# Row groups of 1, 3, 4 and 8 row tiles in place of 4, 6 and 6 in the first projection of a hybrid decoder block

## The chip, the cores and the metric

The kernel runs on one core of a Trainium2 chip. The time is device microseconds of one execution, from launch to the last write; the profile's span runs from the first to the last instruction of one execution that the hardware profiler recorded. Engines: PE (matrix multiplication; PEld are its weight loads), DVE (vector), ACT (scalar), POOL (GpSimd), SP (issues most of the DMA transfers). Each engine runs its own instructions in order and waits on semaphores for the others.

## The reference

One decoder block on x (256 x 2048, float32), with a conditioning vector c. What matters here is its start:

```python
c_act = jax.nn.silu(c)
mod = c_act @ w_ada + b_ada                      # 2048 -> 6 * 2048
sh1, sc1, g1, sh2, sc2, g2 = jnp.split(mod, 6)
h = rms_norm(x, norm_mix_g) * (1.0 + sc1) + sh1
proj = h @ w_in                                  # 2048 -> 8192
u, q, k, v, ga, gb = jnp.split(proj, [1024, 2048, 3072, 4096, 6144])
```

Behind it come an S5 state-space branch on u, attention on q, k and v, a merge gated by sigmoid(ga) and sigmoid(gb), a projection w_out, a second modulated norm, and an MLP of 2048 x 8192 with squared ReLU; at the end a last norm. Everything is float32; the output is 256 x 2048.

## The kernel before

Matrix products keep float32 accuracy by splitting: a weight tile (128 rows of the matrix by 1024 columns, 512 KB) is loaded into `wraw`, ACT casts it to `whi` (L161) and DVE subtracts to get the rest, `wlo` (L163). The activations are split in the same way (`ah`, `al`; the trace calls both `ah`). Three matmuls then make one product: high by high (L208, L261), high by the activations' low (L209, L263), low by high (L210, L265). `wraw` has 7 buffers, `whi` and `wlo` have 4 each, so a cast of weight tile n waits for PE to be done with tile n - 4. `stream` (L167) gives out the split tiles of a unit one after the other.

The rows of w_in are cut into 16 row tiles of 128, which stand for 128 channels of h each. A row tile of h (`make_h1`, L495: `htmp` on ACT, then a split into `ah`) can only be made when its 128 columns of sc1 and sh1 are known: sums over c_act times w_ada. For row tiles 0 to 3 these sums are matmuls (`ada_first`, L272: four loads of 512 KB, tiles named `adap` and `adac` in the trace, a column of `A` and one of `B`). For row tiles 4 to 15 they are wide sums on DVE (`ada_wide`, L351, recorded at L367; tile `ahm`, 128 x 2048, two loads each), four for a pair of row tiles. There are 24 of them. The buffers go round: from the thirteenth on, the load of a wide sum may start when the sum two before it has ended (the table `free`).

So that PE needn't wait for all of h, the first stage is cut into units: a unit is one block of 1024 output columns (0: q, 1: k, 2: v, 3: u, 4: the first half of ga) over the row tiles of one or two groups, accumulated in four PSUM banks. `GR` gives the sizes of the groups. A unit over a later group starts from what the earlier one left: its four banks are emptied by copies (L1066) and the next unit of that block is seeded by four copies back into PSUM (`seeded`, L192). Five banks go round between the units. `gemm_t` (units 0, 1, 3) and `gemm_n` (2, 4) run the matmuls; a row tile of a unit is called a tile here, and the stage has 80 of them, 0 to 79. At the end of each tile, `step` (L138) runs the side work that stands in lanes: "second" (row tiles 1 to 3), "ada" (wide sums), "xr" (scaling x), "ssm" (tables of the state-space branch on DVE, ACT and PE). `want` (L1110) runs out of turn what is needed for the next row tile.

With (4, 6, 6) the units are q, k, v, u over row tiles 0 to 3, ga over 0 to 9, u, v, k over 4 to 9, q over 4 to 15, and ga, u, k, v over 10 to 15. In the first unit each of the row tiles 1 to 3 is made between two tiles of q (`follow`, L1022), and eight matmuls that nobody reads (`idle`, L126, tile `unread`) run while its input is made.

The program is written once and ordered by a list scheduler with priorities (`high_priority`) and extra order edges (`after`); so the order on each engine is that of the built program, shown below.

Of the kernel before, what the change touches and what calls it, by code (L numbers as in the profile page):

```python
# [41 lines left out]
OF1 = 3000  # L42
# [13 lines left out]
RS3 = .7  # L56
GR = (4, 6, 6)
RAT = 1.5
# [19 lines left out]
class Kern:  # L78
    def __init__(self, ctx, tc, a, out):
# [14 lines left out]
        self.done = []  # L94
        self.want = lambda kt: None

    def hot(self):
# [69 lines left out]
    def stream(self, src, kts, c0, homes=()):  # L167
        homes = list(homes)
        for kt in kts:
# [17 lines left out]
            self.step()  # L187

    def seeded(self, banks, seed):
        for o, d in zip(banks, seed or ()):  # L190
            with self.tc.high_priority(offset=OFF):
                self.nc.scalar.copy(*d(o))  # L192
        return bool(seed)

    def gemm_t(self, src, kts, c0, xh, xl, koff=0, mid={}, homes=(), seed=None):
        nc = self.nc
        banks = self.four("pt")
        full = self.seeded(banks, seed)
        n = len(kts)
        for i, (kt, hi, lo) in enumerate(self.stream(src, kts, c0, homes)):  # L200
            kx = kt - koff
# [38 lines left out]
    def gemm_n(self, src, kts, c0, xh, xl, koff=0, tail=1, mid={}, homes=(), seed=None):  # L240
# [4 lines left out]
        held, prev = [], None  # L245
        for i, unit in enumerate(self.stream(src, kts, c0, homes)):
            u = (i,) + unit
# [689 lines left out]
    def body(self):  # L937
# [52 lines left out]
        def modn(kt, home=None, gates=(None, None)):  # L990
            return (self.ada_first(1, kt, fin_scale(1, A1, lambda: self.gmix, kt, 1), home and home[0:2], gates[0]),
                    self.ada_first(0, kt, fin_shift(0, B1, kt, 1), home and home[2:4], gates[1]))

        def totals(parts):
            for units, fold, last in parts:
                for ld, tot in units:
                    tot()
            for units, fold, last in parts:
                fold(parts[1][2]())
# [20 lines left out]
        homes = {1: regs[0:4], 2: regs[4:8], 3: [h[:, i, :] for h in h4 for i in range(2)]}  # L1020

        def follow(kt):  # L1022
            def f():
                with self.tc.high_priority(offset=OF1):
                    parts = modn(kt, homes[kt], (self.mid, self.mm))
                    for units, fold, last in parts:
                        for ld, tot in units:
                            ld()
                    self.scale1(kt, n=1)
                    totals(parts)  # L1030
                    self.idle(8)
                    self.make_h1(kt, A1, B1, 1)
                    self.gates = [(None, self.acopy)] + ([(None, self.done[-1][1])] * 3 if kt == 3 else [])
            return f
        self.early = False
        self.qk = self.slot("S1", [P, 2, 8, S], name="qk")
# [52 lines left out]

        def qkvu(which, g0, g1):  # L1090
            kts = range(groups[g0][0], sum(groups[g1]))
            c0 = (1024, 2048, 3072, 0, 4096)[which]
            f = self.gemm_n if which in (2, 4) else self.gemm_t
            evac(which, f(win, kts, c0, self.ah, self.al, seed=seeds(which) if g0 else None), g0)

# [33 lines left out]
        self.drain = drain  # L1129
        self.lane("second", [follow(kt) for kt in (1, 2, 3)], 1.0)  # L1130
        self.lane("xr", [nop] * 3 + [lambda k0=k0: self.scale1(k0, self.done[-1][0]) for k0 in range(4, KT, 2)], .5)
        jobs = self.ringed(units, free)
        self.lane("ada", [nop] * 3 + jobs[0:1] + [nop] * 2 + jobs[1:] + late, R1)
        self.lane("ssm", [nop] * SL + self.ssm_builds(), 1.0)
        for u in ((0, 0, 0), (1, 0, 0), (2, 0, 0), (3, 0, 0), (4, 0, 1), (3, 1, 1), (2, 1, 1), (1, 1, 1), (0, 1, 2),
                  (4, 2, 2), (3, 2, 2)):
            qkvu(*u)
            if u == (4, 0, 1):
                self.lanes["ssm"][1] = SR1
# [4 lines left out]
        self.bias_load()  # L1144
        qkvu(1, 2, 2)
        qkvu(2, 2, 2)
        ga = self.ga
# [390 lines left out]
```

## Time and profile before

| | us |
|---|---|
| median of 3 runs (lowest, highest) | 1383.23 (1383.08, 1383.5) |
| the profiled execution | 1383.14 |
| its span | 1381.3 |
| PE, DVE, ACT busy | 1352.4, 1043.7, 741.1 |
| end of q's unit (tile 55 of the 80) | 202.9 |
| mean granted clock of PE | 0.996 |

A row of the order of time gives the start and the length in us, the engine, the line, the operation with output and inputs, the shapes, the count and, in brackets, how long the engine sat idle before it and what ended that. A row of a stretch gives the bounds, the length, each engine's busy time with its count of instructions, the granted clock of PE (1.00 is full), the share of the DMA engines and GB/s. A row of the waits gives who waited for whom: the total, the number and the longest in us.

### The profile page before, as it was taken

To read this page: it belongs to the slowest core of one execution; us is meant where nothing else is said; L and a number is where in the kernel's file an instruction comes from. 1 tells how busy PE (TensorE), PEld (TensorE's weight loads), DVE (VectorE), ACT (ScalarE), POOL (GpSimd) and SP (SyncE) were. 2 spreads that over 40 slices of the span, in tenths; PEclk is the share of its full clock that TensorE was granted. 3 is DMA by queue.
4 is the path that set the end of the run, shared out by engine and by line. 5 is a ranking of instruction groups with operands and counts; after the bars stand their busy time and mean duration, and the time that the engine had idled before them with its cause. 6 is when DMAs were issued, how large, how long until landed. Compare 5 with 4: busy or idle time off the path is not lost.

```text
span 1381.3 us, 21633 instructions
## 1 busy us (share of the span) xinstructions
PE 1352.4 (98%) x8338; PEld 1173.9 (85%) x8338; DVE 1043.7 (76%) x1449; ACT 741.1 (54%) x1020; POOL 42.6 (3%) x96
## 2 busy tenths in 40 slices
PE   6999999999999999999999999999999999999997
PEld 5888899988888887888999888888888888888885
DVE  6699987687898898988886976777666555555676
ACT  4466658656557643446565655444453554634543
POOL 1000000500003000000000000000000000000000
PEclk9999999999999999999999999999999999999999
DMA  9999965898447889898697878788878656566561
GB/s 371 387 400 371 354 206 176 263 333 280 164 160 235 298 294 341 294 391 290 212 361 242 284 248 251 244 251 286 246 240 242 200 189 197 188 190 195 179 202 64
DMA packets 112423, 356.43 MB, mean 258 GB/s; under 512 B 12240, under 2 KB 12272, under 8 KB 111904
## 3 DMA queue, kind: packets, MB, share of 16 engines
q1 hardware_dynamic: 109280, 348.96, 74.5%
q0 software_dynamic: 2896, 5.83, 1.4%
q8 instruction: 65, 1.06, 0.3%
q10 hardware_dynamic: 144, 0.26, 0.1%
q14 instruction: 38, 0.31, 0.1%
HBM read 350.79 MB, written 2.51 MB: 256 GB/s over the span
## 4 chain that ended last, share of the span: by engine, by line
PE 59%; DVE 3%; DMA 1%; ACT 1%; issue 1%; DVEq 0%; ACTq 0%
PE pd L226 13%; PE pn L261 11%; PE pn L263 11%; PE pn L265 11%; PE pd L230 7%; PE pt L208 2%; PE pt L210 2%; PE pt L209 2%; DVE wraw L325 1%; DMA wraw<-in_w_proj_ssm_dram 1%; DVE wlo L163 1%; DMA wraw<-in_w_out_dram 0%; DMA wraw<-in_w_ff_dram 0%; ACT whi L161 0%; PE trm L1232 0%
## 5 line engine op out<-in xcount | busy, mean ns | idle before, releaser
L161 ACT CAST whi<-wraw 128x1024 fp32r<-128x1024 f32 x448 | 467.6, 1051 | 516.7 <-PE pn L263 228.4
L163 DVE TENSOR_TENSOR wlo<-wraw,whi 128x1024 fp32r<-128x1024 f32 x448 | 545.2, 1223 | 253.4 <-ACT whi L161 248.5
L226 PE MATMUL pd<-h2h,whi 128*128 128x512 f32 x800 | 208.9, 393 | 0.0
L261 PE MATMUL pn<-whi,ff 128*128 128x512 f32 x496 | 193.0, 389 | 0.0
L263 PE MATMUL pn<-whi,ff 128*128 128x512 f32 x496 | 193.0, 389 | 0.0
L265 PE MATMUL pn<-wlo,ff 128*128 128x512 f32 x496 | 191.6, 389 | 0.0
L226 PEld LDWEIGHTS pd<-h2h,whi 128*128 128x128 f32 x800 | 140.5, 189 | 21.7
L325 DVE SCALAR_TENSOR_TENSOR wraw<-wraw,cb 128x1024 f32<-128x1024 f32 x128 | 156.2, 1221 | 0.0
L261 PE MATMUL pn<-whi,ah 128*128 128x512 f32 x320 | 126.3, 397 | 2.3 <-ACT ah L161 1.6
L230 PEld LDWEIGHTS pd<-h2h,wlo 128*128 128x128 f32 x800 | 116.1, 190 | 12.5
L263 PE MATMUL pn<-whi,ah 128*128 128x512 f32 x320 | 125.2, 391 | 0.0
L230 PE MATMUL pd<-h2h,wlo 128*128 128x256 f32 x800 | 119.3, 281 | 0.0
L265 PE MATMUL pn<-wlo,ah 128*128 128x512 f32 x320 | 115.1, 393 | 0.0
L208 PE MATMUL pt<-ah,whi 128*128 128x256 f32 x384 | 106.3, 287 | 6.4 <-ACT ah L161 4.7
L265 PEld LDWEIGHTS pn<-wlo,ff 128*128 128x128 f32 x496 | 93.1, 188 | 19.4
L261 PEld LDWEIGHTS pn<-whi,ff 128*128 128x128 f32 x496 | 93.1, 188 | 19.2
L263 PEld LDWEIGHTS pn<-whi,ff 128*128 128x128 f32 x496 | 93.1, 188 | 19.0
L209 PE MATMUL pt<-ah,whi 128*128 128x256 f32 x384 | 108.3, 287 | 0.0
L210 PE MATMUL pt<-ah,wlo 128*128 128x256 f32 x384 | 103.4, 285 | 0.0
L208 PEld LDWEIGHTS pt<-ah,whi 128*128 128x128 f32 x384 | 73.2, 194 | 7.6 <-ACT ah L161 5.4
L209 PEld LDWEIGHTS pt<-ah,whi 128*128 128x128 f32 x384 | 74.2, 193 | 1.3 <-issue 0.8
L261 PEld LDWEIGHTS pn<-whi,ah 128*128 128x128 f32 x320 | 60.0, 188 | 15.0 <-ACT ah L161 1.8
(378 smaller groups left out, 2016.8 us busy)
## 6 DMA issues: line engine op xcount, KB each, us to landing
wraw<-in_w_ff_dram SPq DMA_DIRECT2D x256, 512.0 KB, 4.8
wraw<-in_w_in_dram SPq DMA_DIRECT2D x128, 512.0 KB, 6.3
wraw<-in_wat_dram SPq DMA_DIRECT2D x128, 512.0 KB, 5.6
ahm<-in_wat_dram SPq DMA_DIRECT2D x48, 512.0 KB, 7.2
wraw<-in_w_out_dram SPq DMA_DIRECT2D x32, 512.0 KB, 6.4
wraw<-in_w_proj_attn_dram SPq DMA_DIRECT2D x16, 512.0 KB, 6.2
wraw<-in_w_proj_ssm_dram SPq DMA_DIRECT2D x16, 512.0 KB, 6.0
ahm<-in_wan_dram SPq DMA_DIRECT2D x8, 512.0 KB, 11.6
```

The source lines that it names most:

```text
L161: h = self.nc.scalar.copy(hi, src)
L163: s = self.nc.vector.tensor_sub(lo, src, hi.bitcast(F32))
L208: nc.tensor.matmul(o, hi[:, c], xh[:, kx, :], start=st, stop=False, skip_group_check=True)
L209: nc.tensor.matmul(o, hi[:, c], xl[:, kx, :], start=False, stop=False, skip_group_check=True)
L210: self.mm = nc.tensor.matmul(o, lo[:, c], xh[:, kx, :], start=False, stop=sp, skip_group_check=True)
L226: nc.tensor.matmul(banks[blk], hi[:, cut(blk, k)], x2[:, ks[k], :, :], start=i + k == 0, stop=False, skip_group_check=True)
L230: self.mm = nc.tensor.matmul(banks[blk][:, S:2 * S], lo[:, cut(blk, k)], x2[:, ks[k], 0, :], start=False, stop=last and k == 1, skip_group ...
L261: nc.tensor.matmul(o, xh[:, kx, tk], hi[:, c], start=q == 0 and not full, stop=False, skip_group_check=full)
L263: nc.tensor.matmul(o, xl[:, kx, tk], hi[:, c], start=False, stop=False, skip_group_check=full)
L265: self.mm = last = nc.tensor.matmul(o, xh[:, kx, tk], lo[:, c], start=False, stop=q == n - 1, skip_group_check=full)
L325: v.scalar_tensor_tensor(w, w, 1.0, self.cb[:, (i % 2) * 1024:(i % 2 + 1) * 1024], op0=OP.mult, op1=OP.mult, accum_out=pc[:, i:i + 1])
```

## The change

The groups are now 1, 3, 4 and 8 row tiles. Five units begin on the first row tile: q, k, v, u over row tile 0 alone (tiles 0 to 3) and ga over row tiles 0 to 3 (tiles 4 to 7). Then u, v, k over row tiles 1 to 3 (8 to 16), q over 1 to 7 (17 to 23), k, v, u over 4 to 7 (24 to 35), ga over 4 to 15 (36 to 47), and q, u, k, v over 8 to 15 (48 to 79). There are 17 units in place of 13, and twelve of them are seeded in place of nine. The making of row tiles 1 to 3 is spread: `follow` sums, `finish` folds and makes the row tile a tile later; the unread matmuls are gone. And `prime` takes the next unit's first weight tile (load and split) ahead of the copies that empty the banks of the unit before.

```diff
-GR = (4, 6, 6)
+GR = (1, 3, 4, 8)
+    def prime(self, *args):
+        gen = self.stream(*args)
+        self.primed = (next(gen), gen)
+
+    def flow(self, *args):
+        if self.primed:
+            first, gen = self.primed
+            self.primed = None
+            yield first
+        else:
+            gen = self.stream(*args)
+        yield from gen
 ...
-        for i, (kt, hi, lo) in enumerate(self.stream(src, kts, c0, homes)):
+        for i, (kt, hi, lo) in enumerate(self.flow(src, kts, c0, homes)):
 ...
+        sums = {}
+
         def follow(kt):
             def f():
                 with self.tc.high_priority(offset=OF1):
-                    parts = modn(kt, homes[kt], (self.mid, self.mm))
-                    for units, fold, last in parts:
-                        for ld, tot in units:
-                            ld()
+                    sums[kt] = modn(kt, homes[kt], (self.mid if kt < 3 else self.mm, self.mm))
+                    for i in range(2):
+                        for units, fold, last in sums[kt]:
+                            for job in units:
+                                job[i]()
+            return f
+
+        def finish(kt):
+            def f():
+                with self.tc.high_priority(offset=OF1):
+                    for units, fold, last in sums[kt]:
+                        fold(self.mm)
                     self.scale1(kt, n=1)
-                    totals(parts)
-                    self.idle(8)
                     self.make_h1(kt, A1, B1, 1)
-                    self.gates = [(None, self.acopy)] + ([(None, self.done[-1][1])] * 3 if kt == 3 else [])
             return f
 ...
+        def qkvu(u, after=None):
+            which, g0, g1 = u
             f = self.gemm_n if which in (2, 4) else self.gemm_t
-            evac(which, f(win, kts, c0, self.ah, self.al, seed=seeds(which) if g0 else None), g0)
+            banks = f(*place(*u), self.ah, self.al, seed=seeds(which) if g0 else None)
+            if after:
+                self.prime(*place(*after))
+            evac(which, banks, g0)
 ...
-        self.lane("second", [follow(kt) for kt in (1, 2, 3)], 1.0)
+        self.lane("second", [follow(1), both(finish(1), follow(2)), finish(2), nop, follow(3), finish(3)], 1.0)
 ...
-        for u in ((0, 0, 0), (1, 0, 0), (2, 0, 0), (3, 0, 0), (4, 0, 1), (3, 1, 1), (2, 1, 1), (1, 1, 1), (0, 1, 2),
-                  (4, 2, 2), (3, 2, 2)):
-            qkvu(*u)
-            if u == (4, 0, 1):
+        order = [(0, 0, 0), (1, 0, 0), (2, 0, 0), (3, 0, 0), (4, 0, 1), (3, 1, 1), (2, 1, 1), (1, 1, 1), (0, 1, 2),
+                 (1, 2, 2), (2, 2, 2), (3, 2, 2), (4, 2, 3), (0, 3, 3), (3, 3, 3)]
+        for u, after in zip(order, order[1:] + [None]):
+            qkvu(u, after)
+            if u == (0, 1, 2):
                 self.lanes["ssm"][1] = SR1
 ...
-        qkvu(1, 2, 2)
-        qkvu(2, 2, 2)
+        qkvu((1, 3, 3), (2, 3, 3))
+        qkvu((2, 3, 3))
```

The order on the engines, at three places. A row has the line, the operation, output and inputs, and the shape; x2 stands for two in a row. Line numbers of the changed kernel are 14 to 30 higher.

PE, before, between the first unit's row tiles 0 and 1 (q in banks `pt_341` to `pt_344`): the second half of the sums, the two folds, the unread matmuls, and q's row tile 1.

```order
L210 MATMUL pt_344<-ah,wlo 128x256
L295 MATMUL adap<-ahm,tz_70 32x128 x16
L305 MATMUL adac<-s_69 128x1 x2
L130 MATMUL unread<-whi 128x256 x8
L208 MATMUL pt_341<-ah,whi 128x256
```

PE, after, at the same place, and at the end of k's only tile (`pt_425` to `pt_428`), which follows q's.

```order
L309 MATMUL adap<-ahm,tz_70 32x128 x16
L222 MATMUL pt_425<-ah,whi 128x256
...
L224 MATMUL pt_428<-ah,wlo 128x256
L319 MATMUL adac<-s_69 128x1 x2
L309 MATMUL adap<-ahm,tz_70 32x128 x32
L275 MATMUL pn_515<-whi,ah 128x512
```

The sums of row tile 1 are followed by k's tile, the folds come behind it, then the sums of row tile 2 and v's tile.

ACT, before, at the change from k over row tiles 4 to 9 (`pt_1619` to `pt_1622`) to q (`pt_1825` to `pt_1828`): copies that empty (L1066), copies that seed (L192), and one cast between.

```order
L1066 COPY qk<-pt_1619 128x512
L1066 COPY qk<-pt_1620 128x512
L192 COPY pt_1826<-qk 128x512
L192 COPY pt_1827<-qk 128x512
L1066 COPY qk<-pt_1621 128x512
L161 CAST whi<-wraw 128x1024
```

ACT, after, at the change from k over row tiles 1 to 3 (`pt_927` to `pt_930`) to q (`pt_1042` to `pt_1045`). The first cast is that of tile 18; the last row makes row tiles 6 and 7.

```order
L1090 COPY qk<-pt_927 128x512
L1090 COPY qk<-pt_928 128x512
L206 COPY pt_1043<-qk 128x512
L1090 COPY qk<-pt_929 128x512
L206 COPY pt_1044<-qk 128x512
L1090 COPY qk<-pt_930 128x512
L206 COPY pt_1045<-qk 128x512
L162 CAST whi<-wraw 128x1024
L206 COPY pt_1304<-qk 128x512
L162 CAST whi<-wraw 128x1024
L514 ACTIVATE htmp<-xt,B_114,A_113 128x256 x2
L162 CAST ah<-htmp 128x2x256
```

Seven copies stand ahead of that cast, and tiles 18 and 19 are cast ahead of row tiles 6 and 7.

DVE, before, around the last two of the 24 wide sums (L367), which belong to row tiles 14 and 15: the low halves (L163) are those of tiles 47 and 48, 49 to 51, and 52 and 53; the last row is the low half of row tiles 14 and 15, first used by tile 54.

```order
L367 SCALAR_TENSOR_TENSOR ahm,pw<-ahm,cb 128x2048
L163 TENSOR_TENSOR wlo<-wraw,whi 128x1024 x2
L663 TENSOR_TENSOR bp<-tt 128x32x16
L663 TENSOR_TENSOR tt<-bp,AB 128x512
L367 SCALAR_TENSOR_TENSOR ahm,pw<-ahm,cb 128x2048
L163 TENSOR_TENSOR wlo<-wraw,whi 128x1024 x3
L976 TENSOR_TENSOR B_114<-pw,cols 128x2
L163 TENSOR_TENSOR wlo<-wraw,whi 128x1024 x2
L163 TENSOR_TENSOR ah<-htmp,ah 128x2x256
```

DVE, after, the same two sums: the low halves are those of tile 47 and of tiles 48 and 49.

```order
L381 SCALAR_TENSOR_TENSOR ahm,pw<-ahm,cb 128x2048
L164 TENSOR_TENSOR wlo<-wraw,whi 128x1024
L381 SCALAR_TENSOR_TENSOR ahm,pw<-ahm,cb 128x2048
L164 TENSOR_TENSOR wlo<-wraw,whi 128x1024 x2
L990 TENSOR_TENSOR B_114<-pw,cols 128x2
L164 TENSOR_TENSOR ah<-htmp,ah 128x2x256
```

Row tiles 14 and 15 are ready two to four tiles of weights earlier than before, and are first used by tile 46, eight tiles earlier; on PE only twelve matmuls of the unit behind (q, tiles 48 and 49 in its first bank) stand between tile 45 and tile 46.

More of the change, by code (lines that the diff above doesn't have):

```diff
@@ L187, in stream @@
             self.step()
+    def prime(self, *args):
[4 more added lines that the diff above has]
+            first, gen = self.primed
+            self.primed = None
+            yield first
+        else:
+            gen = self.stream(*args)
+        yield from gen
     def seeded(self, banks, seed):
@@ L245, in gemm_n @@
         held, prev = [], None
-        for i, unit in enumerate(self.stream(src, kts, c0, homes)):
+        for i, unit in enumerate(self.flow(src, kts, c0, homes)):
             u = (i,) + unit
@@ L1024, in f, with both @@
                 with self.tc.high_priority(offset=OF1):
-                    parts = modn(kt, homes[kt], (self.mid, self.mm))
-                    for units, fold, last in parts:
-                        for ld, tot in units:
-                            ld()
+                    sums[kt] = modn(kt, homes[kt], (self.mid if kt < 3 else self.mm, self.mm))
[9 more added lines that the diff above has]
+                        fold(self.mm)
                     self.scale1(kt, n=1)
-                    totals(parts)
-                    self.idle(8)
                     self.make_h1(kt, A1, B1, 1)
-                    self.gates = [(None, self.acopy)] + ([(None, self.done[-1][1])] * 3 if kt == 3 else [])
             return f
+        def both(*fs):
+            return lambda: [f() for f in fs]
         self.early = False
@@ L1088, in body, with place @@
                           + mod2(1) + mod2(2) + mod2(3))
-        def qkvu(which, g0, g1):
-            kts = range(groups[g0][0], sum(groups[g1]))
-            c0 = (1024, 2048, 3072, 0, 4096)[which]
+        def place(which, g0, g1):
+            return win, range(groups[g0][0], sum(groups[g1])), (1024, 2048, 3072, 0, 4096)[which]
+        def qkvu(u, after=None):
+            which, g0, g1 = u
             f = self.gemm_n if which in (2, 4) else self.gemm_t
-            evac(which, f(win, kts, c0, self.ah, self.al, seed=seeds(which) if g0 else None), g0)
+            banks = f(*place(*u), self.ah, self.al, seed=seeds(which) if g0 else None)
+            if after:
+                self.prime(*place(*after))
+            evac(which, banks, g0)
         ready = [0, 2]
```

## The prediction, made before the changed kernel ran

> **What bounds the kernel now.** I read the page's first part, then the stretches, then who waited for whom, then single rows in order of time. Tiles are counted 0 to 79 in the order in which this stage uses the 512 KB pieces of w_in.
>
> ```profile
> PE 1352.4 (98%) x8338; PEld 1173.9 (85%) x8338; DVE 1043.7 (76%) x1449; ACT 741.1 (54%) x1020; POOL 42.6 (3%) x96
> PE pt L208 <- ACT ah L161: 4.7, 4, 3.3
> PE pt L208 <- ACT pt L192: 1.7, 1, 1.7
> PE pn L261 <- ACT ah L161: 1.6, 1, 1.6
> ```
>
> PE is the bound over the whole: 29 us of the span are without it. What the change can win is PE's waits up to the end of w_in, and matmuls that nobody reads. The waits for ah are for row tiles of the modulated input: 3.3 us for the first, three of 0.45 in the front, 1.6 for row tile 8; the 1.7 is a seed of a unit's bank.
>
> The average hides a second bound:
>
> ```profile
> 55.40:106.20 50.80, 50.80 (x302) 45.14 (x301) 50.77 (x58) 29.04 (x38) 0.00 (x0) 1.00 1.01 387
> 98.31 2.29 DVE L367 SCALAR_TENSOR_TENSOR ahm<-ahm,cb 128x2048 f32<-128x2048 f32 x1
> 100.53 1.22 DVE L163 TENSOR_TENSOR wlo<-wraw,whi 128x1024 fp32r<-128x1024 f32 x1
> 101.67 2.29 DVE L367 SCALAR_TENSOR_TENSOR ahm<-ahm,cb 128x2048 f32<-128x2048 f32 x1
> 103.88 2.36 DVE L163 TENSOR_TENSOR wlo<-wraw,whi 128x1024 fp32r<-128x1024 f32 x2
> 105.33 0.39 PE L261 MATMUL pn<-whi,ah 128*128 128x512 f32 x1
> 105.56 0.39 PE L263 MATMUL pn<-whi,ah 128*128 128x512 f32 x1
> ```
>
> In a stretch the figures are PE, PEld, DVE, ACT, POOL, clock, DMA. From 55.4 to 106.2 DVE is busy 50.77 of 50.80 us and the DMA engines 1.01: wide sums of w_ada (start to next start 2.21) and low halves of weight tiles (1.14). The split that begins at 103.88 is tile 23's, done at 105.0; PE begins tile 23 at 105.33 and wants its low half by about 105.8. So PE runs less than 1 us behind DVE there, and whatever it wins before is lost again unless DVE comes sooner too.
>
> **The front.**
>
> ```profile
> 30.51 0.84 PE L305 MATMUL adac<-s 128*128 128x1 f32 x4
> 31.21 1.19 PE L130 MATMUL unread<-whi 128*128 128x256 f32 x8
> 32.84 0.75 PE L208 MATMUL pt<-ah,whi 128*128 128x256 f32 x4 [0.45 <-ACT ah L161]
> 40.62 0.75 PE L208 MATMUL pt<-ah,whi 128*128 128x256 f32 x4 [0.45 <-ACT ah L161]
> ```
>
> A row tile takes 40.62 - 32.84 = 7.78 us, of which 32.84 - 31.21 = 1.63 pass with unread matmuls and the wait for its input. Three times that is 4.9 us that the change takes away, since k, v and u of row tile 0 are there to run. The adap sums and adac stay. One wait returns: row tile 3's B stands on DVE behind the second wide sum. By the durations of these rows the first wide sum starts near 49.2 (after tile 8's low half), the second ends at 53.85, B, htmp 0.6 and the cast 0.4 give ah at 55.1, and PE has run out at 53.75: 1.4 us. Net 3.5 here.
>
> **Where it goes.** DVE's work up to tile 23's low half is the same, and its first wide sum starts at 49.2 in place of 55.4: 6 us sooner. But ACT must now empty and seed banks for units of three row tiles.
>
> ```profile
> 132.96 0.61 ACT L192 COPY pn<-v 128x512 f32<-128x512 f32 x1
> 133.48 0.60 ACT L1066 COPY uT<-pt 128x512 f32<-128x512 f32 x1
> 107.35 1.06 ACT L161 CAST whi<-wraw 128x1024 fp32r<-128x1024 f32 x1 [1.66 <-PE pn L263]
> 108.30 1.09 ACT L500 ACTIVATE htmp<-xt,B,A 128x256 f32<-128x256 f32 x2
> 109.42 0.62 ACT L161 CAST ah<-htmp 128x512 fp32r<-128x512 f32 x1
> 110.10 1.20 PE L261 MATMUL pn<-whi,ah 128*128 128x512 f32 x4 [1.65 <-ACT ah L161]
> ```
>
> A copy takes 0.52 to the next start, eight to a seeded unit (4.2 us), a cast 0.95. ACT takes them in the order shown above: tile 18's cast stands behind seven copies that wait for the banks of the unit before it. Laid end to end with these durations, DVE waits for casts of tile 11 (0.8), 12 (2.3), 18 (1.3) and for row tile 6's ah (0.5): 4.9 us, with PE held 1.1 by seeds near 59. So tile 23's low half comes at 104.2, not 105.0, and PE ends tile 23 about 106.1.
>
> Then a gain that stays: tile 24 needs row tile 0, no longer row tile 8, so PE does not wait as it does at 110.10. It starts tile 24 at 106.1, 4.0 us sooner. The seed wait of 1.7 at 150 belongs to a unit that is cut otherwise: up to 1.9 more. Of the twelve seeded units (nine before) I find none after tile 23 in which PE waits for a copy; by the rows a change of unit costs between 0 and 1.9.
>
> **The new wait.** Row tile 14 is first needed by tile 46 in place of tile 54, while its four wide sums keep their places among the splits. Rows of before, DVE, ACT and the DMA issue:
>
> ```profile
> 165.44 2.28 DVE L367 SCALAR_TENSOR_TENSOR ahm<-ahm,cb 128x2048 f32<-128x2048 f32 x1
> 167.76 0.80 SPq L361 DMA_DIRECT2D ahm<-in_wat_dram  x2
> 177.76 2.28 DVE L367 SCALAR_TENSOR_TENSOR ahm<-ahm,cb 128x2048 f32<-128x2048 f32 x1
> 179.97 3.49 DVE L163 TENSOR_TENSOR wlo<-wraw,whi 128x1024 fp32r<-128x1024 f32 x3
> 183.38 0.15 DVE L976 TENSOR_TENSOR B<-pw,cols 128x2 f32<-128x2 f32 x1
> 187.80 0.62 ACT L161 CAST ah<-htmp 128x512 fp32r<-128x512 f32 x1
> DMA to landing us min/median/max: 4.5/7.0/10.3
> 202.81 0.28 PE L210 MATMUL pt<-ah,wlo 128*128 128x256 f32 x1
> 202.93 0.40 PE L261 MATMUL pn<-whi,ah 128*128 128x512 f32 x1
> ```
>
> The last wide sum (177.76) reads a buffer that the sum two before it (165.44) must free: its load is issued at 167.76, as that one ends. Before, row tile 14's ah stands at 188.4 and tile 54 starts at 202.93 - 2 x 2.88 = 197.2 (24 matmuls, 0.12 apart, to a tile of this form): 8.8 us to spare. After, PE's time without a wait: tile 24 at 106.1, then 8 tiles of 2.88 and 14 of 2.74 (12 matmuls, 0.228 apart): tile 45 ends at 167.5. DVE's: from 104.2, 24 low halves of 1.14, eleven sums of 2.21, three low halves of ah at 0.61, ten products of the SSM build at 0.6, 1 us of small ones, and 3 for casts and landings: the last sum could start at 168. But its load waits for the sum two before, which ends near 163.1; with 7.0 to land, 170.1. Then the sum 2.21, low halves of tiles 48 and 49 2.27, B 0.15, htmp 1.1, ah 0.65: 176.5. PE has only half a tile to fill in (twelve matmuls of tiles 48 and 49, whose low halves come after that sum too). Before, 46 and a half tiles were done at 202.93 - 9.5 x 2.88 = 175.6. So all that was won is gone: +0.9.
>
> DVE being quicker helps little: the sum two before the last stands behind tile 45's low half, whose cast needs the buffer that tile 41 leaves (four buffers; the cast at 107.35 shows such a wait). Tile 41 ends at 156.5. Cast, low half, ah, sum: 4.6; the shortest landing 4.5; then 6.4: 172.0 at best.
>
> **The clock.**
>
> ```profile
> 19.44:22.77 3.33, 0.00 (x1) 0.01 (x1) 3.26 (x19) 2.73 (x6) 0.00 (x0) 0.82 1.02 402
> 22.77:28.40 5.63, 5.63 (x48) 4.93 (x49) 3.72 (x27) 0.27 (x1) 0.00 (x0) 0.50 1.03 410
> 106.20:120.00 13.80, 12.15 (x71) 10.61 (x71) 13.71 (x20) 8.75 (x14) 1.31 (x2) 1.00 0.98 345
> ```
>
> After 3.33 us without PE the clock is 0.50 for 5.63 us more: 2.8 us of work lost. The wait of 1.65 at 108 leaves it at 1.00. The wait at tile 46 is some 8 us with half a tile in it, so I add 2.8; the bounds are 0 (the wait too broken) and the 2.8 with the wait's own phase, 3.5. [...]
>
> **Sum.** The profiled execution took 1383.14 us (span 1381.3; median of the runs 1383.23). +0.9 + 2.8 = +3.7: **1386.8**. What follows tile 80 is the same work, PE-bound, and I cost it at nothing: the SSM build is pushed out a few tiles earlier there, in DVE blocks of up to 5 us that the four buffered tiles cover.
>
> **Rivals.**
> 1. Not slower: row tile 14 comes at the best time, 172.0, with no half clock: 172.0 - 175.6 = -3.6, 1379.5. The last load's landing decides: 4.5 in place of 7.0, and DVE without backlog at tile 45. For it: DVE is not full after 140. Against: weights are queued ahead of that load, and the median was 7.0 in this stage. Without any wait at tile 46 it would be 167.5 against 174.1, 1376.5.
> 2. The same wait, the clock kept: 1384.0. It decides by how the half tile breaks the gap.
> 3. ACT is late at the short units: five of the seven changes of unit between tiles 4 and 28 hold PE 1.9 as the one at 150 does, 1390 or more. For it: ACT has 8 copies and 3 casts, 7.1 us, in a unit of 8.6. Against: only one of nine seeded changes shows it now.
> 4. It does not do what it says: the row tiles 1 to 3 hold PE as before. Then tile 41 is late by up to the 4.0, and the chain behind it too: 1390.
>
> **Chances.** Forecast (1385 to 1389) 0.5, almost all of it slower; rival 1 0.17; rival 2 0.18; rivals 3 and 4 0.15. What a measurement can tell from no change is about 0.2%, 2.8 us: below 1380.4 is faster, above 1385.9 slower. Faster: most of rival 1, 0.14. Same: rival 2, the near ends of the forecast and of rival 1, 0.3. Slower 0.56. The range: landing 10.3 in place of 7.0 gives +3.3 and rival 3 lies there, 1391; the other end is rival 1's, 1379.
>
> **What would show it.** Right: no unread matmuls, no wait of 0.45 between row tiles 0 and 2; a wait of 1 to 2 us for row tile 3's ah near 54; DVE full from 50 to 110 but for waits on casts; no wait at tile 24; then PE idle for 5 us or more near 170 on ah, and a clock of 0.5 behind it. Wrong: no such wait, or DVE over 3 us ahead of before at tile 23, which would leave more of the front's gain; or many waits for seed copies, which would be rival 3.

## The result, and the profile after

The changed kernel takes 1392.7 us (median of 4 runs, 1391.66 to 1394.4), the kernel before 1383.37 (4 runs, 1383.08 to 1383.7): ratio 1.0069, 95% interval 1.0051 to 1.0086. It is slower, as forecast, but by 9.3 us in place of 3.6, and outside the range (1379 to 1391). The profiled execution took 1391.66 us, its span is 1389.9: 8.5 over the profiled one of before.

First the page's line of busy times and the costliest waits of PE (who waited for whom; total, times, longest). The 6.4 lies before the first matmul, as 6.7 did before; the 3.5 is the first row tile's.

```profile
PE 1354.8 (97%) x8314; PEld 1173.4 (84%) x8314; DVE 1045.5 (75%) x1449; ACT 758.2 (55%) x1052; POOL 42.6 (3%) x96
PE pt L224 <- DVE wlo L164: 8.0, 4, 6.9
PE ss L494 <- DVE junk L492: 6.4, 1, 6.4
PE pt L222 <- ACT ah L162: 3.5, 1, 3.5
PE pn L275 <- ACT ah L162: 1.5, 2, 1.0
PE pn L275 <- ACT ga L1213: 1.3, 1, 1.3
PE pav L828 <- ACT ga L821: 0.8, 1, 0.8
```

The three waits of 0.45 and the 1.6 and 1.7 of before are gone. In their place stand one of 6.9 and longer waits for the attention (`ga`, L1213, L821 and, with 0.5, L812; before there was one of 0.6). The length of a wait is PE's idle time, as in the brackets; where "start to start" is said, it is the time between the starts of two matmuls less what they take without a wait, some 0.2 to 0.3 us more for each wait. Now the stretches (bounds, length, PE, PEld, DVE, ACT, POOL, clock, DMA):

```profile
55.40:106.20 50.80, 49.64 (x359) 46.15 (x358) 45.39 (x51) 37.96 (x59) 0.80 (x1) 1.00 1.02 397
106.20:120.00 13.80, 13.24 (x98) 12.10 (x97) 12.45 (x14) 11.18 (x19) 0.52 (x1) 1.00 1.01 403
120.00:168.30 48.30, 48.28 (x259) 41.75 (x258) 43.74 (x50) 29.93 (x44) 0.00 (x0) 1.00 1.00 364
168.30:178.50 10.20, 2.82 (x13) 2.32 (x11) 6.34 (x8) 2.68 (x5) 0.00 (x0) 0.76 0.62 220
178.50:183.80 5.30, 5.28 (x12) 4.13 (x13) 5.16 (x8) 1.20 (x3) 0.00 (x0) 0.50 0.23 84
345.80:351.00 5.20, 2.61 (x11) 1.50 (x10) 2.86 (x8) 4.84 (x15) 0.00 (x0) 1.00 0.01 2
351.00:354.50 3.50, 3.50 (x10) 2.71 (x9) 1.31 (x2) 3.47 (x7) 0.00 (x0) 0.51 0.00 0
```

PE runs almost without a gap from 55 to 168.3. Then it works 2.82 of 10.20 us, and 5.30 more at half clock. A second such place, which the prediction does not have, is at 345.8: half of 5.2 us without PE, and 3.5 us at half clock. How the first came about, by the order of time (DVE, PE, the DMA issue):

```profile
161.55 2.28 DVE L381 SCALAR_TENSOR_TENSOR ahm<-ahm,cb 128x2048 f32<-128x2048 f32 x1
163.87 0.81 SPq L375 DMA_DIRECT2D ahm<-in_wat_dram  x2
166.56 2.29 DVE L381 SCALAR_TENSOR_TENSOR ahm<-ahm,cb 128x2048 f32<-128x2048 f32 x1 [1.32 <-DMA ahm<-in_wat_dram]
171.99 2.29 DVE L381 SCALAR_TENSOR_TENSOR ahm<-ahm,cb 128x2048 f32<-128x2048 f32 x1 [1.99 <-DMA ahm<-in_wat_dram]
174.21 2.35 DVE L164 TENSOR_TENSOR wlo<-wraw,whi 128x1024 fp32r<-128x1024 f32 x2
175.48 0.58 PE L224 MATMUL pt<-ah,wlo 128*128 128x256 f32 x1 [6.86 <-DVE wlo L164]
178.52 2.07 PE L275 MATMUL pn<-whi,ah 128*128 128x512 f32 x4 [0.54 <-ACT ah L162]
```

The sum two before the last ends, the last sum's load is issued at 163.87, the sum starts at 171.99, 8.1 us later; the low halves of tiles 48 and 49 stand behind it, and tile 46 starts at 178.52.

The table shows where the time went. It gives the us at which PE begins the n-th tile of the stage, counted in the trace by matmuls (24 to a tile of 256 columns, 12 to one of 512; where units change, matmuls of two tiles mix, so it is good to about 0.3 us, and up to tile 80 the kernels take tiles of both kinds in different order).

| | tile 24 | 44 | 48 | 80 | span |
|---|---|---|---|---|---|
| before | 108.1 | 168.4 | 179.9 | 284.3 | 1381.3 |
| after | 105.3 | 162.8 | 185.2 | 289.4 | 1389.9 |

The kernel before then waits 1.65 us at tile 24, so the lead there is 4 to 5 us; at tile 44 it is 5.6. At tile 48 it has become a lag of 5.3, which stays to tile 80 (5.1). The rest, 3.5, comes later.

### The profile page after: what moved, and what is told of

It reads as the page before. It is cut to its first block, busy times and chain, and to the rows that moved or that the text cites. A ratio compares the mean times of both kernels' runs of the same rounds, so it can differ in the third digit from the quotient of the medians.

```text
span 1389.9 us, 21608 instructions
## 1 busy us (share of the span) xinstructions
PE 1354.8 (97%) x8314; PEld 1173.4 (84%) x8314; DVE 1045.5 (75%) x1449; ACT 758.2 (55%) x1052; POOL 42.6 (3%) x96
## 4 chain that ended last, share of the span: by engine, by line
PE 83%; DVE 7%; ACT 4%; DMA 3%; issue 2%; SPq 0%; ACTq 0%; DVEq 0%
PE pn L275 15%; PE pn L277 15%; PE pn L279 15%; PE pd L240 13%; PE pd L244 7%; PE pt L224 5%; PE pt L222 5%; PE pt L223 5%; DVE wlo L164 2%; ACT whi L162 1%; DMA wraw<-in_w_proj_ssm_dram 1%; DVE ahm L381 1%; DVE wraw L339 1%; DMA ahm<-in_wat_dram 1%; PE rk L748 1%
## 5 line engine op out<-in xcount | busy, mean ns | idle before, releaser
L162 ACT CAST whi<-wraw 128x1024 fp32r<-128x1024 f32 x448 | 467.4, 1052 | 511.8 <-PE pn L277 224.7
L277 PE MATMUL pn<-whi,ah 128*128 128x512 f32 x320 | 126.6, 396 | 0.0
L222 PEld LDWEIGHTS pt<-ah,whi 128*128 128x128 f32 x384 | 73.8, 193 | 6.5 <-ACT ah L162 3.6
L224 PEld LDWEIGHTS pt<-ah,wlo 128*128 128x128 f32 x384 | 71.7, 194 | 8.2 <-DVE wlo L164 8.1
## 6 DMA issues: line engine op xcount, KB each, us to landing
ahm<-in_wan_dram SPq DMA_DIRECT2D x8, 512.0 KB, 11.4
```

Source lines behind the costliest of these rows:

```text
L162: h = self.nc.scalar.copy(hi, src)
L222: nc.tensor.matmul(o, hi[:, c], xh[:, kx, :], start=st, stop=False, skip_group_check=True)
L224: self.mm = nc.tensor.matmul(o, lo[:, c], xh[:, kx, :], start=False, stop=sp, skip_group_check=True)
L277: nc.tensor.matmul(o, xl[:, kx, tk], hi[:, c], start=False, stop=False, skip_group_check=full)
```

## The experiments

Theory: two losses. At tile 46 row tile 14 is needed before the wide sums can bring it, and in that wait the clock falls to 0.50 (173.56 to 183.80); and the attention runs late, since its first softmax now stands behind casts that wait for PE. Rivals are named with each run. The times are medians, the ratios are to runs of the kernel before on the same chip.

| run | us (runs) | ratio, 95% interval |
|---|---|---|
| e1 pace 0.75 | 1384.22 (11) | 1.0011, 1.0001 to 1.0020 |
| e2 softmax first | 1388.15 (6) | 1.0043, 1.0030 to 1.0055 |
| e3 gap filled | 1391.82 (6) | 1.0064, 1.0050 to 1.0078 |
| e4 no prime | 1392.83 (6) | 1.0076, 1.0059 to 1.0093 |
| e5 needed by tile 54 | 1381.94 (11) | 0.9999, 0.9990 to 1.0008 |
| e6 needed by tile 62 | 1382.37 (11) | 0.9998, 0.9989 to 1.0006 |
| e7 pace 0.65 | 1389.69 (5) | 1.0055, 1.0042 to 1.0067 |
| e8 four buffers | 1389.76 (2) | 1.0048, 1.0031 to 1.0065 |
| e9 four buffers, 0.75 | 1388.92 (5) | 1.0037, 1.0025 to 1.0049 |
| e10 e5 with e9 | 1385.87 (12) | 1.0020, 1.0011 to 1.0029 |
| e11 e6, pace 0.50 | 1381.49 (11) | 0.9989, 0.9980 to 0.9998 |
| e12 e5, front filled | 1381.49 (11) | 0.9990, 0.9981 to 0.9999 |
| e13 before, front filled | 1388.34 (5) | 1.0037, 1.0024 to 1.0049 |
| e14 e11, front filled | 1383.61 (11) | 1.0008, 0.9999 to 1.0017 |
| e15 after, front filled | 1392.49 (5) | 1.0073, 1.0059 to 1.0086 |

### The attention (e2)

The rows of ACT at the start of the attention, in the kernel before and then in the changed one (L795 and L809 are the same line, the exponential of the softmax):

```profile
269.05 1.28 ACT L795 ACT_TABLE_LOAD   x1
271.31 0.41 ACT L795 ACTIVATE ga<-ga,ast 128x128 f32<-128x128 f32 x1 [0.98 <-DVE ast L793]
274.47 2.94 ACT L161 CAST whi<-wraw 128x1024 fp32r<-128x1024 f32 x3
279.50 0.48 ACT L807 COPY ga<-ptr 128x384 f32<-128x384 f32 x1
```

```profile
274.19 2.96 ACT L162 CAST whi<-wraw 128x1024 fp32r<-128x1024 f32 x3 [5.14 <-PE pn L277]
278.50 1.06 ACT L162 CAST whi<-wraw 128x1024 fp32r<-128x1024 f32 x1 [1.35 <-PE pn L277]
280.87 0.40 ACT L809 ACTIVATE ga<-ga,ast 128x128 f32<-128x128 f32 x1
293.83 0.50 ACT L821 COPY ga<-ptr 128x384 f32<-128x384 f32 x1
```

Both start the scores at about the same time (268). Before, ACT does the softmax while it would be idle, and the casts follow. After, four casts stand ahead; ACT sits 5.14 us on PE for a buffer, and the softmax starts 9.6 us later. In e2 the two heads are put back ahead of the cast:

```diff
 ...
-        qkvu((2, 3, 3))
 ...
+        def heads():
+            self.attn1(0)
+            self.attn1(1)
+            self.gates = [(None, None)] * 3 + [(self.arec, self.alast)]
+
+        qkvu((2, 3, 3), mid={0: heads})
...
-        self.lane("m", self.attn_jobs() + [start], RAT, 1.0)
+        self.lane("m", self.attn_jobs()[2:] + [start], RAT, -1.0)
```

> The changed kernel, with the scores and softmax of heads 0 and 1 held ahead of the cast and low half of the last unit's fifth tile, as they stand in the kernel before; nothing ahead of 265 us differs. Theory (the second loss is that the softmax stands behind casts which wait for PE, so that PE runs dry at the end of the heads): the waits of 3.5 us and the half clock at 345 to 354 go, less the 1.0 us of waits which the kernel before has there: -3 to -5, 1388 to 1390. Rival (that loss follows from coming 5.5 us late to this stage, or from the last unit of v having eight tiles): no change, 1392 to 1393.

Measured: 1388.15, ratio 1.0043 against 1.0069. The end of the heads in the kernel before, then both stretches of the changed kernel, then of e2:

```profile
340.00:346.00 6.00, 5.36 (x26) 4.05 (x25) 2.35 (x3) 5.97 (x12) 0.00 (x0) 1.00 0.31 87
```

```profile
344.00:350.00 6.00, 3.87 (x19) 2.39 (x17) 4.13 (x12) 5.15 (x16) 0.00 (x0) 1.00 0.24 95
350.00:356.00 6.00, 5.55 (x19) 4.42 (x20) 1.31 (x2) 5.97 (x12) 0.00 (x0) 0.72 0.00 0
```

```profile
344.00:350.00 6.00, 5.22 (x25) 3.92 (x24) 4.15 (x5) 5.97 (x10) 0.00 (x0) 1.00 0.50 165
350.00:356.00 6.00, 6.00 (x34) 4.92 (x33) 0.00 (x0) 2.41 (x5) 0.03 (x1) 1.00 0.33 122
```

The theory holds: PE's waits fall to one of 0.78, and the half clock is gone. The rival (no change) falls. By the ratios this is 3.6 us of the loss, by the medians 4.6. In the profiles the time from tile 80 to the end is 1097.0 us before, 1100.5 in the changed kernel and 1096.0 in e2.

### Row tile 14 (e1, e7, e8, e9)

```diff
-R2 = .56
+R2 = .75
```

> One number of the changed kernel differs: the pace of the wide sums after row tile 8 is 0.75 a tile in place of 0.56. The last wide sum then stands behind the low half of tile 42 in place of 47; by this build's order the softmax of the first two heads also stands ahead of the next cast again, as in the kernel before. Theory (the loss is the chain behind the last sum's load, with the half clock behind it, and the late softmax): the wait at tile 46 falls from 10 us to under 1.5, no clock of 0.5 near 175, tile 47 ends near 176 in place of 186.5, and the waits at 345 to 354 go: 1378 (1376 to 1381). Rival A (DVE is the bound of this stage, not the landing): sums moved forward hold back low halves, PE waits for wlo in tiles 25 to 42 by as much: 1390 to 1394. Rival B (the attention loss has nothing to do with the softmax's place): 1381 to 1383.

Measured: 1384.22, above the theory and rival B, below rival A. The wait at tile 46 is gone, but PE now waits before it. PE's waits between 104 and 172, and the rows at the change to `ga`:

```profile
PE pn L275 <- ACT pn L206: 3.4, 6, 1.2
PE pt L224 <- DVE wlo L164: 0.7, 3, 0.3
145.72 0.50 PE L275 MATMUL pn<-whi,ah 128*128 128x512 f32 x1 [0.26 <-ACT pn L206]
147.67 0.80 PE L275 MATMUL pn<-whi,ah 128*128 128x512 f32 x1 [1.23 <-ACT pn L206]
147.50:151.00 3.50, 3.33 (x8) 2.68 (x9) 3.50 (x5) 1.69 (x3) 0.00 (x0) 0.51 0.92 309
165.18 2.29 DVE L381 SCALAR_TENSOR_TENSOR ahm<-ahm,cb 128x2048 f32<-128x2048 f32 x1 [1.63 <-DMA ahm<-in_wat_dram]
```

PE stands at the seeds (three waits of 0.2, 0.3 and 1.2 us at each of two changes) and falls to half clock for 3.4 us. My reading is that with more sums ahead of the low halves there is less split weight in stock; the rows show the waits, not this reason. Tile 44 begins at 169.8, 7.0 later than in the changed kernel, tile 48 at 180.8, 4.4 earlier. So Rival A is partly right: of 11.4 us won at tile 46, 7.0 are paid ahead. The rest of what e1 wins lies behind tile 80 (1094.6 us to the end in place of 1100.5), where its softmax starts ahead of the casts again (268.51). The last sum still waits for its load, so I next tried a smaller step, and four buffers.

e7 has the pace 0.65.

> The changed kernel with the pace of the wide sums at 0.65 in place of 0.56 (0.75 was tried). At 0.75 the loads, each waiting for the sum two before it and taking 6 to 8 us to land, held DVE, and PE waited 5 us in seeds and low halves at 118 to 148 in place of 8 at tile 46. The last sum stands behind the low half of tile 45 (47 in the changed kernel, 42 at 0.75). Theory (the sums are paced by their loads' landing, so that each us gained at tile 46 is paid for on DVE before it): between the two, 1384 to 1389, with a wait of 3 to 6 us at tile 46. Rival (0.75 only overshot; a little faster is free): 1381 or less.

Measured: 1389.69, a little above the theory's span. Tile 44 at 166.8, tile 48 at 185.1, with the clock at half for 6.83 us around tile 46 and for 3.41 from 132.8, the end of a wait of 2.3. A little faster is not free; the rival falls.

e8 keeps 0.56 and takes the ring of two away:

```diff
-SL = 18
-SR1 = .27
+SL = 24
+SR1 = 0
...
-        ring = wide * 3 + wide[2:4] * 6
+        ring = wide * 6
...
-        free.update({i: (i + 4,) for i in range(8)})
-        free.update({i: (i + 2,) for i in range(10, 22)})
+        free.update({i: (i + 4,) for i in range(20)})
```

> The changed kernel with four buffers for all wide sums (a load waits for the sum four before it, not two) and, since those buffers are then held longer, the tables of the state-space branch held back until row tile 14 is made. The pace stays 0.56. To be read at tile 46 only: the tables held back come out later and will make the attention late. Theory (the last sum waits for its load, whose issue waits for the sum two before): the last sum's load lands before 165, the sum starts as DVE comes free, near 167, and tile 46 starts near 174 in place of 178.5, with a wait of 5 to 7 us in place of 10. Rival (DVE has so much work before it that landing hides nothing): the sum starts at 171 or later, tile 46 at 178 or later. The whole: 1388 to 1394.

Measured, the waits of DVE between 104 and 172 in the changed kernel and then in e8, and the last sum of e8:

```profile
DVE ahm L381 <- DMA ahm<-in_wat_dram: 6.3, 4, 2.0
```

```profile
DVE wlo L164 <- ACT whi L162: 11.2, 6, 3.9
152.69 0.80 SPq L375 DMA_DIRECT2D ahm<-in_wat_dram  x2
171.24 2.28 DVE L381 SCALAR_TENSOR_TENSOR ahm<-ahm,cb 128x2048 f32<-128x2048 f32 x1
177.45 1.20 PE L275 MATMUL pn<-whi,ah 128*128 128x512 f32 x4
```

The load is issued 11 us earlier, and no sum waits for a load. Yet the last sum starts at 171.24 in place of 171.99, and tile 46 (the last row) at 177.45 in place of 178.52. That is the rival on the sum (171 or later); tile 46 lies between. DVE's waits for loads became waits for casts, which wait for a buffer that PE must leave, and PE is late in this run: tile 44 begins at 167.3 in place of 162.8. Of these 4.5 us, 1.7 are a longer half clock in the front (6.83 us, 3.41 in the changed kernel), 1.65 a wait for a low half at 94, the rest seeds and casts. PE's pause ahead of tile 46, with the twelve matmuls in it, is less than half as long (173.1 to 177.45; in the changed kernel 168.6 to 178.52), the clock stays at 1.00 in it, and tile 48 begins at 182.9 in place of 185.2. So the landing was a part of that pause, but PE comes to it 4.5 us later and tile 46 gains 1.07; how much the landing is worth with the same front stays open. The whole, 1389.76, isn't read, since the tables held back make the attention late.

e9 is e8 with the pace 0.75.

> As the run before, with the pace at 0.75. At 0.75 and two buffers DVE stood on landings (sums 13, 14, 18, 19, 22, 23 started 0.1 us after their load landed) and PE waited 5 us at 118 to 148. Theory (it is the landing in the ring of two that makes the sums dear): no sum waits for its load, no wait over 1 us on PE between 100 and 200, no clock of 0.5 there: 1376 to 1380. Rival (DVE is short of time as such: 1.14 and 0.75 x 2.21 a tile of 2.8): PE waits of 3 us or more for wlo or seeds at 118 to 150 remain, 1381 to 1385.

Measured: 1388.92, neither. No sum waits for its load and tile 46 does not wait, but PE waits 1.65 for a low half at 93, 1.45 for a seed at 131, and 3.86 at 248 for the tables that were held back, with 3.41 us of half clock behind that. So the whole does not judge the theory. Tile 48 begins at 178.7, 1.2 ahead of the kernel before; at tile 24 (107.1) the lead was 2.6. From tile 24 to tile 48 PE takes 71.6 us here, 74.9 in e1 with two buffers at the same pace, 80.0 in the changed kernel, and 70.2 before (without its wait at tile 24). So the landing was about 3 us of the price of the faster pace, unless the tables, which left DVE in this stretch, account for it; the two are not separated. That the rest is DVE's time (between tiles 24 and 48 twelve sums and 24 low halves need it, and whichever comes first, PE pays for the other) is argued, not shown: DVE still waits 9 us for others between 104 and 172.

### A later need (e5, e6, e10, e11)

So the sums were left alone, and the need was moved: groups 1, 3, 4, 4, 4, with ga over row tiles 4 to 15 behind k and v over 8 to 11.

```diff
-GR = (1, 3, 4, 8)
+GR = (1, 3, 4, 4, 4)
...
-                 (1, 2, 2), (2, 2, 2), (3, 2, 2), (4, 2, 3), (0, 3, 3), (3, 3, 3)]
+                 (1, 2, 2), (2, 2, 2), (3, 2, 2), (1, 3, 3), (2, 3, 3), (4, 2, 4), (0, 3, 4), (3, 3, 4)]
...
-        qkvu((1, 3, 3), (2, 3, 3))
-        qkvu((2, 3, 3))
+        qkvu((1, 4, 4), (2, 4, 4))
+        qkvu((2, 4, 4))
```

> Groups of 1, 3, 4, 4, 4: up to tile 35 as in the changed kernel, then k and v over row tiles 8 to 11 (tiles 36 to 43), ga over 4 to 15 (44 to 55), q and u over 8 to 15, k and v over 12 to 15. The pace of the wide sums stays 0.56; row tile 14 is first needed by tile 54, as before the change, and 14 units are seeded in place of 12. The softmax of the first heads stands ahead of the next cast by this build's order. Theory (the loss is the late last sum under an earlier need, and the late softmax; the front's gain is real): no wait over 1 us on ah and no clock of 0.5 between 100 and 300, tile 24's gain of 4 is kept but for 1 to 2 of seeds: 1377 to 1381, below the kernel before. Rival A (units of four row tiles cost PE seed waits wherever they stand, 1.9 each for the two added and more): 1383 to 1388. Rival B (DVE's backlog comes out as a wait elsewhere): waits for wlo of 4 us in sum, 1383 to 1385.

Measured: 1381.94, ratio 0.9999; the profiled span is 1379.4. The stretches that answer to those of the changed kernel:

```profile
120.00:168.30 48.30, 46.38 (x293) 41.61 (x292) 41.95 (x48) 35.92 (x57) 0.00 (x0) 1.00 0.97 349
168.30:198.00 29.70, 29.70 (x133) 24.58 (x132) 27.75 (x30) 15.68 (x20) 0.00 (x0) 1.00 0.72 242
166.50 0.50 PE L279 MATMUL pn<-wlo,ah 128*128 128x512 f32 x1 [1.67 <-DVE wlo L164]
```

No wait on ah behind 54, no half clock, tile 48 at 176.4, 3.5 ahead of before. This removes 1.0069 - 0.9999 = 0.70% or 9.7 us, all that the change had lost against the kernel before; the front's lead doesn't show in it. The time is 0.9 above the theory's span, and what remains of Rival B is one wait of 1.67 for a low half behind a sum.

e6 needs row tile 14 by tile 62: q and u too go over row tiles 8 to 11 ahead of ga.

> As the run before, but q, k, v and u all go over row tiles 8 to 11 (tiles 36 to 51) ahead of ga over 4 to 15 (52 to 63), and all over 12 to 15 behind it: row tile 14 is first needed by tile 62, sixteen units are seeded. Theory: nothing more is won by an even later need, since that wait is gone already; two more seeds: 0 to 2 us above the run before. Rival A (seeds cost): 2 to 4 us above it. Rival B (the wide sums are still late for tile 54): 2 us or more below it.

Measured: 1382.37, 0.4 above e5: nothing more is won, as the theory says; seeds cost nothing that can be seen.

e10 joins e5 with e9's buffers and pace.

> Both cures: groups 1, 3, 4, 4, 4 (row tile 14 first needed by tile 54), four buffers, pace 0.75, tables held back until row tile 14. Theory: the wait of 1.8 at 164 of the earlier run with these groups (low half behind a sum that waits for its cast) goes too: 1376 to 1380, 2 to 4 below that run; if landing was all, no better than the run before this one. Rival (two more seeded units and the tables pushed together cost as much): 1381 to 1384.

Measured: 1385.87, beyond the rival. PE waits 1.65 at 94, 1.45 at 131 and 2.40 at 169, where it is a cast (L162) that is late. Once the need is late, buffers, pace and late tables together only cost; which of the three does is not separated.

e11 goes the other way: e6 with `R2 = .50` and e2's edit.

> The groups 1, 3, 4, 4, 4 with row tile 14 first needed by tile 62, and the pace of the wide sums after row tile 8 at 0.50 in place of 0.56; the first heads' softmax held ahead of the cast as in the build with 0.56. The last sum then stands behind the low half of tile 51 in place of 48. Theory (a faster pace puts sums ahead of low halves that PE needs, so a slower one is better once the need is late enough): the wait of 2.0 for a low half at 176 goes, tile 60 begins at 210 to 211 in place of 212.5, the whole 1379.5 to 1381.5. Rival (that wait is of the four split buffers and a cast, not of the sums): it stays or moves, 1382 to 1383.

Measured: 1381.49, ratio 0.9989, at the upper edge of the theory's span, not told apart from e5 and e6. The wait for a low half (1.86 in e6) is gone; three waits for seeds, 1.45 at 129, 0.99 at 178 and 0.79 at 242, take its place.

### The clock (e3, e12 to e15)

```diff
+    def warm(self, n):
+        o = self.aux("unread")[:, 0:S]
+        with self.tc.high_priority(offset=OF1):
+            for _ in range(n):
+                with self.after(self.mm):
+                    self.nc.tensor.matmul(o, self.ah[:, 0, 0:P], self.ah[:, 0, :], start=True, stop=True)
...
-            qkvu(u, after)
+            qkvu(u, after, {10: lambda: self.warm(64)} if u == (4, 2, 3) else {})
```

> The changed kernel, with 64 matmuls that nobody reads (128x256 on row tile 0, about 7.7 us) between tiles 45 and 46, so that PE is busy for most of the wait. Theory (half of the wait's price beyond its length is the clock): tile 46 starts at 178.5 as before, the clock there stays at 1.00, the work up to 184 takes 2.6 us less: 1390 (the attention loss may gain or lose its 1.7 of half clock by the phase). Rival (the half clock costs nothing, since DVE sets the pace there): 1392 to 1393.

Measured: 1391.82, not told apart from the changed kernel. The stretches (to be read beside those of the changed kernel) and the PE row behind:

```profile
168.30:178.50 10.20, 10.20 (x82) 9.97 (x81) 6.71 (x8) 2.00 (x3) 0.00 (x0) 1.00 0.62 218
178.50:183.80 5.30, 4.69 (x23) 3.71 (x22) 4.33 (x7) 3.41 (x7) 0.00 (x0) 1.00 0.40 148
186.65 0.39 PE L231 MATMUL pt<-ah,wlo 128*128 128x256 f32 x1 [1.32 <-DVE wlo L171]
```

The clock stays at 1.00, so it was the idle PE that lowered it there. But a new wait of 1.32 for a low half follows: DVE is behind by then, and gives back about half of the 2.65 us that the half clock cost. In the profiles tiles 44 to 80 take 125.3 us in place of 126.6, so the clock's own part of the loss is about 1.3 us there; the times of the runs are too close to show it.

e12 to e15 fill the idle 3.3 us ahead of the first row tile in the same way, with matmuls of the identity: 24 in e12 (on e5), 14 in e13 (on the kernel before), e14 (on e11) and e15 (on the changed kernel).

```diff
+            o = self.aux("unread")[:, 0:P]
+            for _ in range(14):
+                with self.after(self.adac):
+                    self.nc.tensor.matmul(o, self.ident, self.ident, start=True, stop=True)
```

> The groups 1, 3, 4, 4, 4 with row tile 14 first needed by tile 54 at pace 0.56, and 24 matmuls of the identity with itself that nobody reads in the front, where PE is idle for 3.3 to 3.6 us before the first row tile and the clock then falls to 0.50 for 3.4 to 6.8 us. Theory (an idle PE, not the work itself, lowers the clock): the clock stays 1.00 from 10 us on, every tile from 4 on begins 1.7 to 3.4 us sooner, and since DVE and the loads there do not move, part of it (0 to 2) is kept at tile 24: 1379 to 1381. Rival (clock falls by itself in the front, or all of the gain is lost on DVE by tile 24): 1381.5 to 1382.5.

> The kernel before with 14 matmuls of the identity that nobody reads (3.3 us: the 24 of the earlier run took 5.5 and made the first row tile late) in the idle time ahead of the first row tile. Theory (that idle time lowers the clock): clock 1.00 to 28, the first row tiles 1.7 to 3.4 sooner; but DVE is full from 55 to 106 there and its first wide sum comes as soon as row tile 3 is made, so about 2 us are kept: 1380 to 1381.5. Rival (DVE and the loads set tile 24 whatever PE does): 1382.5 to 1383.

> The groups 1, 3, 4, 4, 4 with row tile 14 first needed by tile 62 at pace 0.50 and the softmax ahead of the cast, with the same 14 matmuls in the front. Theory (the front's change is worth 1 to 3 us of its own, and the clock's phase is apart from it): 1 to 3 us below the run before, 1378 to 1380. Rival (the lead of 4 us at tile 24 in the profiles was the clock's phase): within 0.5 us of the run before.

> The changed kernel with the same 14 matmuls in the front. Theory (whatever the front wins is lost in the wait at tile 46, since the chain of wide sums does not start earlier than row tile 3 allows): it moves no more than the sums do, 1391 to 1393. Rival (the front's clock is worth as much here as in the kernel before): 2 us below the changed kernel, 1390 to 1391.

Measured: 1381.49 (24 matmuls took 5.5 us and delayed the first row tile), 1388.34, 1383.61, 1392.49. e12 lies at the edge of its rival, e13 and e14 are above both theory and rival. In all four the clock stays at 1.00 there; in e13:

```profile
22.77:28.40 5.63, 5.63 (x93) 4.91 (x91) 4.11 (x28) 0.66 (x2) 0.00 (x0) 1.00 1.03 410
94.51 0.69 DVE L163 TENSOR_TENSOR ah<-htmp,ah 128x512 fp32r<-128x512 f32 x1 [2.62 <-ACT ah L161]
PE pn L261 <- ACT ah L161: 2.8, 1, 2.8
PE pn L265 <- DVE wlo L163: 2.1, 4, 0.9
```

The kernel before has its first tiles 2 us earlier by it and is 5.5 us slower: the scheduler put the wide sums and row tiles in another order, DVE sat 2.62 us on a row tile, and PE waited 2.8 for row tile 8, after which the clock was at half for 3.41 us (from 114.8). e14 is 2.1 us above e11: it too loses what the front wins. e15 is as the theory has it: the front's gain cannot be used where the sums set tile 46. So e13 is no clean base, and what the front is worth by itself stays open.

### The order of the first split (e4)

```diff
-            if after:
-                self.prime(*place(*after))
```

> The changed kernel without its second part: the next unit's first weight tile is split behind the copies that empty the banks, as in the kernel before. My prediction costed that part at nothing. Theory: within 1 us of the changed kernel, 1391.5 to 1393.5. Rival A (splitting ahead holds the banks longer and makes the seeds late): 2 us or more faster. Rival B (it is what keeps PE from waiting for the first tile at the twelve seeded changes): 3 to 10 us slower, 1396 to 1403, with waits for whi or wlo at changes of unit.

Measured: 1392.83, within the noise of the changed kernel. `prime` costs and wins nothing here, as the prediction had it.

## Why the prediction was right in sign and wrong in size

1. **The front.** Right. The unread matmuls and the three waits are gone. Row tile 3's wait came at 52.72, 1.28 from start to start (1.4 at 53.75 forecast); the row of DVE from 55.4 to 106.2 is no longer full (45.39 of 50.80), since DVE waits there 4.8 us for casts and 0.4 for a row tile (4.9 forecast for both).
2. **Tile 24.** Right: it begins at 105.3 without a wait (106.1 forecast), and the seed wait of 1.7 is gone. Seeds after tile 23 cost 0.5 at 118, where I found none. (Eight units are seeded before the change, not nine: L192 copies 32 times, four to a unit. Nothing in the sum hangs on it.)
3. **The new wait.** Right in place and cause of the moment, mis-sized. Tile 45 ends at 168.2 (167.5); the sum two before the last ends at 163.83 (163.1); the load then takes 8.1 to the sum's start in place of 7.0; tile 46 starts at 178.5 in place of 176.5. That is 2.0 too little, 0.7 of it from the end of that sum and 1.1 from the landing; at tile 80 the lag is 5.1 in place of 0.9 + 2.8 = 3.7, so 1.4 of it is left. The sentence that DVE being quicker helps little is borne out in part: e1, e7 and e8 each win at tile 46 and pay most of it ahead, and e9, which wins 6.5 us at tile 48, has lost them by tile 80 (289.9 in place of 289.4) with the wait for the tables that it moves and the half clock behind it.
4. **The clock.** Right in the profile: 5.30 us at 0.50 behind the wait, 2.65 lost, 2.8 forecast; that the size fits is partly luck, for in e4 the clock came back 3.5 us after tile 46 began (177.05 to 180.54). In the traces of before and after the granted clock was at 0.50 for 3.41, 6.83 or 10.24 us at a time (but for the last 5 us of each). In the kernel before it fell at 21.55, when PE had been idle for 2.1 of the 3.33 us: within that wait, not after it. The upper bound of 3.5 on the loss was my estimate; no run shows it. What I missed is that PE, slowed, hides DVE's lag: e3 keeps the clock and wins 1.3 us in the profile.
5. **What follows tile 80.** This is the step that failed: "What follows tile 80 is the same work, PE-bound, and I cost it at nothing". The work is the same, but its order on ACT and DVE is not. The first softmax fell behind four casts, the attention became 9.6 us late where 5.1 were the lag, and PE waited 3.5 us (start to start) and then ran 3.4 us at half clock: 5.2 in place of 0.85, so 4.4. e2 shows it. About 1 us comes back behind the attention (the wait of 1.77 at 474 before is one of 0.75), which leaves 3.5 behind tile 80. With the 1.4 of step 3 that is the 4.9 by which the profiled execution is above the forecast.
6. **The rivals.** Rival 2 (clock kept) is e3's kernel and not this one. Rival 3 (seeds) is hardly seen here (0.5 us at 59 and 0.5 at 118), but appears as soon as the sums are hurried (e1). Rival 1 needed a quick landing and DVE without backlog; e8 gave it the first, but not PE's time at tile 44, and tile 46 moved by 1 us.

Where the front's gain went in the changed kernel: to the need at tile 46. With the need at 54 or 62 the kernel is level with before (0.9999, 0.9998) or 0.1% below it (e11, e12). Why so little is left of 4 us, when the profiles of e5, e6 and e11 still have tile 80 at 282.2 to 282.9 (284.3 before), isn't settled. In e5's profile the lead is 4.8 at tile 24, 3.5 at tile 48, 2.2 at tile 80 and 1.9 at the end; 1.7 of it can be the front's clock, which was at half for 3.41 us in e5 and for 6.83 in the profile of before, and runs of one kernel differ by 2 to 7 us. Why the scheduler put the softmax behind the casts was not tried.

## What to carry to other kernels

When an order table changes, follow every consumer in the order of the built program to the end of the kernel, not only to the end of the stage: a list scheduler gives other engines another order far behind the edit. An operand that is made by a full engine sets the earliest useful place of its first use; here moving that use later was cheap (e5, 0.9999 in place of 1.0069), while making the operand sooner moved most of the wait to an earlier place (e1, 7.0 of 11.4 us). Look also at what a removed wait was hiding before you count it.

## What the runs showed of the hardware

- In the trace of the kernel before, from 20 to 1376 us, the granted clock was 1.00 but for 6.83 us at 0.50 from 21.55. In that of the changed kernel, from 20 to 1385 us, it was 1.00 but for 3.41 us at 0.50 from 23.37, 10.24 from 173.56 and 3.41 from 351.05.
- The length of a wait alone did not tell what it cost in clock. The clock fell 2.1 us into the first row tile's wait of 3.33 (before), but 0.5 us behind the one of 3.55 (after), 4.9 us into the wait of 6.86, and at 351.05 behind waits of 0.46, 0.78 and 1.27. A wait of 2.8 in e13 was followed by 3.41 us at half clock, one of 2.88 in e8 and those of 1.65 and 1.7 in the kernel before by none. What else decides is not shown.
- Filling an idle PE with matmuls that nobody reads held the clock at 1.00 where they stood in all five kernels (in e3 from 168.30 to 183.80, where the changed kernel has 0.76 and 0.50), and made none of them more than 0.1% faster: 1.3 us were given back on DVE (e3), or more in another order (e13).
- In the changed kernel a 512 KB piece of w_ada took 8.1 us from issue to use (163.87 to 171.99, the DMA engines 97% busy), and DVE, busy for 43.74 of the 48.30 us from 120.00 to 168.30, waited 6.3 us for such pieces between 104 and 172.
